# Ten operand sums of each gate and up phase on GpSimd instead of VectorE

## The chip, the cores and the metric

One Trainium2 chip, one of its cores. A core has TensorE for matmuls (PE; its weight loads are PEld), VectorE (DVE), ScalarE (ACT), GpSimd (POOL) and SyncE (SP), which issues most DMAs here. Each engine works through its own queue in order and waits on semaphores for the others. The metric is the time of one execution on the device in microseconds, lower is better, as the median of several runs.

## The reference

One layer of a hybrid decoder trunk on 1024 tokens of width 1024, all in float32:

```python
x = x + 0.5 * swiglu(rms_norm(x, ffn1_norm), ffn1_w_gate, ffn1_w_up, ffn1_w_down)
x = x + hybrid_mixer(rms_norm(x, mix_norm), w_in, ..., w_out)
x = x + 0.5 * swiglu(rms_norm(x, ffn2_norm), ffn2_w_gate, ffn2_w_up, ffn2_w_down)
return rms_norm(x, final_norm)

def swiglu(h, w_gate, w_up, w_down):
    a = jnp.einsum("bld,df->blf", h, w_gate)
    b = jnp.einsum("bld,df->blf", h, w_up)
    return jnp.einsum("blf,fd->bld", jax.nn.silu(a) * b, w_down)
```

The hidden width D_FF is 2816. The mixer (a gated delta rule of 8 heads beside a Mamba-2 scan of 16 heads) lies between the two feed-forward parts and isn't touched.

## The kernel before, in words

**Seven products.** The gate and the up matmul multiply the normalised tokens, 1024 by 1024, by weights of 1024 by 2816. The kernel cuts the tokens' matrix into four blocks (two halves of the tokens, two halves of the width) and a weight tile of 256 columns into four blocks a11, a12, a21, a22. A product of two such block matrices is made with seven block products (numbered m = 1 to 7) instead of eight; the operands of most of them are sums or differences of two blocks. The results are added up in four PSUM banks named c11, c12, c21, c22 in the code.

**High and low parts.** Each operand is split: ScalarE casts it to fp32r (the high part), VectorE subtracts the high part from it (the low part). `split2`, lines 238 to 240, does both, so one operand of 128 x 512 is a cast and a subtraction (L239, L240). A block product, `prod`, runs four steps of k with three matmuls each (L332 high by high, L333 weights' high by tokens' low, L334 weights' low by tokens' high), twelve matmuls of 512 columns.

**Names.** Token operands are `bh` and `bl`, weight operands `ah` and `al`. `wst` is a raw weight tile as loaded, `as` a weight sum, `bs` a token sum, `keepx` the two kept scaled blocks r11 and r22, `m` and `m2f` are products copied from PSUM. H[m] holds the token operand of product m, ops[m] the weight operand.

**The start of a phase.** There are two gate and up phases, one for each feed-forward part: the first starts with the kernel, the second at about 1640 us. Before the steady loop over the 22 weight tiles (11 of gate, 11 of up) a phase has a start in which all token operands are made and the first two weight tiles, one of gate and one of up, are worked on side by side:

- `b_first` (lines 261 to 269) makes the token operands 2 and 4 and keeps r11.
- `a_start` (lines 325 and 326) makes the weight operands of the first two tiles in four groups, by the table A_START: group 0 has products 2 and 4, group 1 products 3 and 6, group 2 products 5 and 7, group 3 product 1, each for both tiles. It calls `a_ops` (lines 304 to 319), where L315 is the sum of two weight blocks.
- `b_second` (lines 271 to 295) makes the token operands 3 and 6, calls `between(0)`, makes 5 (r22 alone, no sum) and 7, calls `between(1)`, and makes 1. Operands 3, 6 and 7 take one block straight from PSUM after a transpose (L279), operand 1 is the sum of the kept r11 and r22, four sums of 128 x 512 (L294).
- `between` is the function f in `start_rest` (lines 669 to 678). f(0) issues the first matmuls (`first_products`: 2, 4 and 3) and group 2 of the weights; f(1) makes group 3 and loads the next two weight tiles.
- `gate_up_all` (from line 352) goes on with products 6, 5, 7 and 1, whose bank is tagged sc, combines the banks, and enters the loop, in which `a_ops` makes the operands of the next tile by A_GROUPS.

**Buffers.** Sums and the two copies `m3` of the third product come from tag "q" of the pool, which has four buffers. The two m3 are filled early in the start and are in use until the banks are combined (lines 384 to 400). Weight operands have two buffers of four operands each, the tags whi and wlo.

**What sets the order.** The code isn't executed in the order in which it is written. A planner in the build goes through the instructions, with the written order as priority, modelled durations, and buffers given out as they come free, and writes out one queue for each engine. `tc.issue_after(ins)` puts the instructions of a block behind `ins` on its engine. In the chip each queue is then strictly in order: an instruction that waits holds everything behind it on its engine. In the second phase, for example, the planned order of TensorE has the fifth product, most of the first, and then the seventh.

Of the kernel before, what the change touches and what calls it, by code (L numbers as in the profile page):

```python
# [16 lines left out]
ALU = mybir.AluOpType  # L17
# [27 lines left out]
def kernel(  # L45
# [7 lines left out]
    V, A, G, T = nc.vector, nc.scalar, nc.gpsimd, nc.tensor  # L53
# [217 lines left out]
    def b_second(pool, x0, x1, wcol, H, r11, r22, between):  # L271

        def operand(m, k, f):
            t = pool.tile([P, 512], F32, name="bs", tag="q")
            f(t)
            return split2(b_op(H, m)[0][:, k], b_op(H, m)[1][:, k], t)

        def scaled(pt, kx, other, op):
            return lambda t: V.scalar_tensor_tensor(out=t, in0=pt, scalar=wcol[:, kx:kx + 1], in1=other,  # L279
                                                    op0=ALU.mult, op1=op)  # L280

        for k in range(4):
            A.mul(out=r22[:, k], in_=transposed(x1, k + 4), mul=wcol[:, k + 4:k + 5])
            p12 = transposed(x1, k)
            operand(3, k, scaled(p12, k, r22[:, k], ALU.subtract))
            operand(6, k, scaled(p12, k, r11[:, k], ALU.add))
        between(0)
        for k in range(4):
            split(b_op(H, 5)[0][:, k], b_op(H, 5)[1][:, k], r22[:, k])
        for k in range(4):  # L290
            operand(7, k, scaled(transposed(x0, k + 4), k + 4, r22[:, k], ALU.add))
        between(1)
        for k in range(4):
            last = operand(1, k, lambda t: V.tensor_tensor(out=t, in0=r11[:, k], in1=r22[:, k], op=ALU.add))  # L294
        return last

    A_GROUPS = ((3, 2, 1, 5), (4, 7, 6))
# [3 lines left out]
        nc.sync.dma_start(out=raw, in_=w.rearrange("(k p) c -> p k c", p=P)[:, :, p * 256:(p + 1) * 256])  # L301
        return raw

    def a_ops(pool, *prods):

        hi = wp.tile([P, 4, 4, P], F32R, name="ah", tag="whi")
        lo = wp.tile([P, 4, 4, P], F32R, name="al", tag="wlo")
        for i, (raw, m, ops) in enumerate(prods):
            a11, a12 = raw[:, 0:4, 0:P], raw[:, 4:8, 0:P]
            a21, a22 = raw[:, 0:4, P:2 * P], raw[:, 4:8, P:2 * P]  # L310
            v = {3: a11, 4: a22, 2: (a21, a22, ALU.add), 1: (a11, a22, ALU.add), 5: (a11, a12, ALU.add),
                 7: (a12, a22, ALU.subtract), 6: (a21, a11, ALU.subtract)}[m]
            if isinstance(v, tuple):
                t = pool.tile([P, 4, P], F32, name="as", tag="q")
                V.tensor_tensor(out=t, in0=v[0], in1=v[1], op=v[2])  # L315
                v = t
            last = split2(hi[:, i], lo[:, i], v)
            ops[m] = hi[:, i], lo[:, i]
        return last


    A_START = (((0, 2), (0, 4), (1, 2), (1, 4)), ((0, 3), (1, 3), (0, 6), (1, 6)),
               ((0, 5), (1, 5), (0, 7), (1, 7)), ((0, 1), (1, 1)))

    def a_start(pool, raws, ops, n):
        a_ops(pool, *((raws[j], m, ops[j]) for j, m in A_START[n]))

    def prod(H, bank, ops, m, first):
        (wh, wl), (bh, bl) = ops[m], H[m]
# [357 lines left out]
    with ExitStack() as c1:  # L687
        npool = NormPool(ffn_pools(c1))
        H = {}
        with tc.tile_pool(name="x1", bufs=1, side="right", reuse_waits="tile") as xp, \  # L690
# [5 lines left out]
            raws = [a_load(ffn1_w_gate[0], 0), a_load(ffn1_w_up[0], 0)]  # L696
            for b in range(4, NB):
                nc.sync.dma_start(out=xt[b], in_=x_v[:, b])
            ops = [{}, {}]
            x0, last = normalise_pairs(npool, xt, "h6")  # L700
            with tc.issue_after(last.ins), tc.issue_after(cols_in.ins):
                a_start(npool, raws, ops, 0)
            r11, r22 = (kp.tile([P, 4, 512], F32, name=f"keepx{i}") for i in range(2))
            with tc.issue_after(last_t.ins):
# [3 lines left out]
            last = b_second(npool, x0, x1, nrm[0], H, r11, r22,  # L708
                     start_rest(npool, H, ffn1_w_gate[0], ffn1_w_up[0], raws, ops))
# [100 lines left out]
    with tc.tile_pool(name="gtmp", bufs=1, side="right", reuse_waits="tile") as tp:  # L810
# [23 lines left out]
        for b in range(NB):  # L834
# [12 lines left out]
                        in1=bias.unsqueeze(1).to_broadcast([P, NB, NG]), op=ALU.add)  # L847
# [11 lines left out]
        for c in (15, 13, 11, 9, 7, 5, 3):  # L859
# [8 lines left out]
                               in1=alog.unsqueeze(1).to_broadcast([P, NB, NG]),  # L868
# [11 lines left out]
                        op=ALU.subtract)  # L880
# [19 lines left out]
    for un in range(4):  # L900
# [37 lines left out]
        for b0 in range(0, NB, 2):  # L938
# [6 lines left out]
            for name, lst, sc in (("xdt", xdts, bc2(dtn, b0)), ("xe", xes, bc2(dxe, b0))):  # L945
                t = s1.tile([P, 2, 256], F32, name=name, tag=name, bufs=4)
                last_x = V.tensor_tensor(out=t.rearrange("p i (h c) -> p i h c", h=4), in0=ptv, in1=sc,
                                         op=ALU.mult)
# [42 lines left out]
        for b0 in range(0, NB, 4):  # L991
# [33 lines left out]
            for b, py, *_ in pairs:  # L1025
                for j in range(2):
                    xv = xst[j][:, b * P:(b + 2) * P]
                    V.scalar_tensor_tensor(out=xv, in0=xv, scalar=dcol[:, 2 * un + j:2 * un + j + 1],
                                           in1=py[:, j * 256:(j + 1) * 256], op0=ALU.mult, op1=ALU.add)
# [71 lines left out]
    with ExitStack() as cg:  # L1101
        g1 = cg.enter_context(tc.tile_pool(name="gdn1", bufs=1, reuse_waits="tile"))
        g2 = cg.enter_context(tc.tile_pool(name="gdn2", bufs=2, reuse_waits="tile"))
        for h in range(GH):
# [31 lines left out]
            for b0 in range(0, NB, 2):  # L1136
# [14 lines left out]
                for i in range(2):  # L1151
# [4 lines left out]
                                in0=pg.rearrange("p (i c) -> p i c", i=2)[:, :, P:2 * P],  # L1156
                                in1=dt[:, b2], op=ALU.mult)
# [24 lines left out]
            for half in range(2):  # L1182
                pt = psum("mx")
                for i in range(4):
# [4 lines left out]
                                in1=rin[:, hb].unsqueeze(2).to_broadcast([P, 4, P]), op=ALU.mult)  # L1189
# [12 lines left out]
            for j in range(31):  # L1202
                r, n = j // 4 + 1, 31 - j
                t = ft[:, 0:r * n].rearrange("p (s l) -> p s l", l=n)
                V.tensor_tensor(out=t, in0=fx[:, 0:r, j:j + 1].to_broadcast([P, r, n]),
                                in1=fu[:, j:j + 1, j + 1:32].to_broadcast([P, r, n]), op=ALU.mult)
# [51 lines left out]
            for half in range(2):  # L1258
                pt = psum("sc")
                for i in range(4):  # L1260
# [4 lines left out]
                                in1=wend[:, hb, h:h + 1].to_broadcast([P, 4, P]), op=ALU.mult)  # L1265
# [3 lines left out]
            for b in range(NB):  # L1269
                bs = slice(b * P, (b + 1) * P)  # L1270
                rr = vr[:, b]
                if st is not None:
# [4 lines left out]
                                           in1=vr[:, b], op0=ALU.mult, op1=ALU.add)  # L1277
# [8 lines left out]
                if b < NB - 1:  # L1286
# [5 lines left out]
                    else:  # L1292
                        V.scalar_tensor_tensor(out=sn, in0=st, scalar=egt[:, b, h:h + 1],
                                               in1=p3[:, 0:P], op0=ALU.mult, op1=ALU.add)
# [100 lines left out]
    raws = [a_load(ffn2_w_gate[0], 0), a_load(ffn2_w_up[0], 0)]  # L1395
    ops = [{}, {}]
# [89 lines left out]
```

## Time and profile before

| | |
|---|---|
| runs | 2311.19, 2312.62, 2313.73 us; median 2312.62 |
| profiled execution | 2311.71 us |
| span of its profile | 2309.8 us, 31485 instructions |
| granted TensorE clock | 0.999 |
| PE busy | 2275.9 us, 99% |
| DVE busy | 1726.7 us, 75% |
| ACT busy | 1096.0 us, 47% |
| POOL busy | 53.6 us, 2% |
| the 220 weight sums L315 (both phases, start and loop) | 145.0 us on DVE, 684 ns each |
| the 8 token sums L294 | 692 ns each |
| GpSimd's largest work, the selections L895 | 36.5 us, 24 of them, all in the mixer |

The span runs from the first to the last instruction; the profiled execution's own time has some 1.9 us more around it. A row of a group gives line, engine, operation, output and inputs, shapes and count, then busy time in us and the mean in ns, then the idle time of the engine just before and what ended it. A row of the timeline gives start and duration in us, then engine, line, operation, and in brackets the idle time before it and its releaser; consecutive equal instructions stand in one row with their count. The matmuls are pipelined: each is shown with 0.39 us, and one starts every 0.23 us when nothing is waited for, so a busy share of TensorE near 100% can still hide holes of a few tenths. Time is lost where the distance between two starts is larger.

### The profile page before, as it was taken

How to read it: one execution, taken by the hardware profiler on the slowest of the kernel's cores; microseconds unless marked ns; L12 is line 12 of the kernel's file. 1: busy time of each engine (PE TensorE's matmuls, PEld its weight loads, DVE VectorE, ACT ScalarE, POOL GpSimd, SP SyncE). 2: the span in 40 equal slices, each digit the busy share in tenths (PEclk: the TensorE clock that was granted, in tenths of full speed). 3: DMA queues.
4: the chain of work that ended last, by engine and by line, in shares of the span. 5: the costliest groups of instructions: out<-in, count | busy, mean ns of one | idle time of the engine just before them, and what ended most of it. 6: DMA issues, size and time to landing. Idle time of an engine off the chain costs nothing.

```text
span 2309.8 us, 31485 instructions
## 1 busy us (share of the span) xinstructions
PE 2275.9 (99%) x11766; PEld 1868.7 (81%) x11766; DVE 1726.7 (75%) x3349; ACT 1096.0 (47%) x1990; POOL 53.6 (2%) x125
## 2 busy tenths in 40 slices
PE   7999999999999999999999999999999999999998
PEld 5788888888878888888888888888878888888886
DVE  7977776767765675668778888778698777766787
ACT  7433333343367785864455556422543333334344
POOL 0000000000000100000000000000000000000000
PEclk9999999999999999999999999999999999999999
DMA  3333332573652322222333222335223333329456
GB/s 111 125 114 103 105 108 98 175 279 129 220 180 78 92 92 74 72 86 74 83 101 82 73 83 61 116 98 192 91 83 116 111 102 105 109 88 349 141 156 214
DMA packets 220957, 281.33 MB, mean 122 GB/s; under 512 B 47008, under 2 KB 153564, under 8 KB 219780
## 3 DMA queue, kind: packets, MB, share of 16 engines
q1 hardware_dynamic: 220548, 279.23, 37.4%
q8 instruction: 92, 1.51, 0.3%
q14 instruction: 61, 0.50, 0.1%
q0 software_dynamic: 256, 0.10, 0.0%
HBM read 211.55 MB, written 67.73 MB: 121 GB/s over the span
## 4 chain that ended last, share of the span: by engine, by line
PE 89%; DVE 5%; ACT 2%; DMA 1%; issue 1%; SPq 0%; POOL 0%; DVEq 0%; ACTq 0%
PE ps_pj L123 11%; PE ps_pj L122 10%; PE ps_pj L121 10%; PE ps_pj L332 6%; PE ps_pj L334 6%; PE ps_pj L333 6%; PE ps_mx L332 3%; PE ps_mx L334 3%; PE ps_mx L333 3%; PE ps_pj L553 2%; PE ps_pj L554 2%; PE ps_pj L552 2%; PE ps_oo L334 2%; PE ps_oo L333 2%; PE ps_oo L332 2%; PE ps_sc L552 1%
## 5 line engine op out<-in xcount | busy, mean ns | idle before, releaser
L123 PE MATMUL ps_pj<-hhi,wlo 128*128 128x512 f32 x832 | 334.3, 402 | 0.0
L121 PE MATMUL ps_pj<-hhi,whi 128*128 128x512 f32 x832 | 332.8, 400 | 0.4 <-ACT gsb L826 0.4
L122 PE MATMUL ps_pj<-hlo,whi 128*128 128x512 f32 x832 | 332.2, 399 | 0.0
L334 PE MATMUL ps_pj<-bh,al 128*128 128x512 f32 x688 | 267.9, 389 | 0.0
L333 PE MATMUL ps_pj<-bl,ah 128*128 128x512 f32 x688 | 267.8, 389 | 0.0
L332 PE MATMUL ps_pj<-bh,ah 128*128 128x512 f32 x688 | 267.5, 390 | 0.0
L121 PEld LDWEIGHTS ps_pj<-hhi,whi 128*128 128x128 f32 x832 | 156.7, 188 | 28.8 <-ACT gsb L826 0.8
L123 PEld LDWEIGHTS ps_pj<-hhi,wlo 128*128 128x128 f32 x832 | 156.7, 188 | 28.5 <-issue 0.7
L122 PEld LDWEIGHTS ps_pj<-hlo,whi 128*128 128x128 f32 x832 | 156.7, 188 | 27.9
L239 ACT CAST ah<-wst 128x512 fp32r<-128x512 f32 x88 | 54.6, 622 | 210.8 <-PE ps_oo L333 125.3
L239 ACT CAST hid<-hraw 128x1024 fp32r<-128x1024 f32 (+1 forms) x84 | 82.3, 981 | 145.5 <-PE ps_oo L554 60.6
L333 PEld LDWEIGHTS ps_pj<-bl,ah 128*128 128x128 f32 x688 | 129.2, 188 | 26.8
L334 PEld LDWEIGHTS ps_pj<-bh,al 128*128 128x128 f32 x688 | 129.1, 188 | 26.6
L332 PEld LDWEIGHTS ps_pj<-bh,ah 128*128 128x128 f32 x688 | 128.9, 188 | 26.6
L315 DVE TENSOR_TENSOR as<-wst 128x512 f32<-128x512 f32 x220 | 145.0, 684 | 2.1 <-DMA wst<-in_ffn_w_up_dram 1.8
L240 DVE TENSOR_TENSOR al<-as,ah 128x512 fp32r<-128x512 f32 x220 | 141.0, 685 | 5.0 <-ACT ah L239 4.5
L332 PE MATMUL ps_mx<-bh,ah 128*128 128x512 f32 x352 | 138.6, 396 | 3.8 <-ACT m L341 1.4
L333 PE MATMUL ps_mx<-bl,ah 128*128 128x512 f32 x352 | 138.2, 393 | 0.4 <-DVE bl L240 0.4
L334 PE MATMUL ps_mx<-bh,al 128*128 128x512 f32 x352 | 137.7, 391 | 0.3 <-DVE al L240 0.3
L239 ACT CAST ah<-as 128x512 fp32r<-128x512 f32 x220 | 125.0, 617 | 20.8 <-DVE as L315 20.8
L240 DVE TENSOR_TENSOR hid<-hraw,hid 128x1024 fp32r<-128x1024 f32 (+1 forms) x84 | 95.0, 1131 | 32.8 <-ACT hid L239 32.5
L341 ACT COPY m<-ps_pj 128x512 f32<-128x512 f32 x88 | 51.5, 588 | 123.1 <-PE ps_pj L334 120.9
(448 smaller groups left out, 5118.9 us busy)
## 6 DMA issues: line engine op xcount, KB each, us to landing
hraw<-hid_scr SPq DMA_DIRECT2D x70, 512.0 KB, 4.4
hid_scr<-hs SPq DMA_DIRECT2D x110, 256.0 KB, 2.3
wst<-in_ffn_w_down_dram SPq DMA_DIRECT2D x50, 512.0 KB, 4.7
wst<-in_ffn_w_gate_dram SPq DMA_DIRECT2D x22, 1024.0 KB, 5.7
wst<-in_ffn_w_up_dram SPq DMA_DIRECT2D x22, 1024.0 KB, 5.4
wst<-in_w_in_dram SPq DMA_DIRECT2D x36, 512.0 KB, 5.2
hid_scr<-sg SPq DMA_DIRECT2D x44, 256.0 KB, 2.0
keep<-in_ffn_w_down_dram SPq DMA_DIRECT2D x20, 512.0 KB, 6.2
```

Source lines behind the costliest of these rows:

```text
L121: T.matmul(o, lhsT=wh, rhs=mh, start=first, stop=False)
L122: T.matmul(o, lhsT=wh, rhs=ml, start=False, stop=False)
L123: T.matmul(o, lhsT=wl, rhs=mh, start=False, stop=last)
L239: return (A.copy(out=hi, in_=src), V.tensor_tensor(out=lo, in0=src, in1=hi.bitcast(F32), op=ALU.subtract))
L240: V.tensor_tensor(out=lo, in0=src, in1=hi.bitcast(F32), op=ALU.subtract))
L315: V.tensor_tensor(out=t, in0=v[0], in1=v[1], op=v[2])
L332: T.matmul(bank, lhsT=wh[:, k], rhs=bh[:, k], start=a, stop=False, skip_group_check=True)
L333: T.matmul(bank, lhsT=wh[:, k], rhs=bl[:, k], start=False, stop=False, skip_group_check=True)
L334: T.matmul(bank, lhsT=wl[:, k], rhs=bh[:, k], start=False, stop=z, skip_group_check=True)
L341: A.copy(out=t, in_=bank)
L552: T.matmul(bank, lhsT=hh, rhs=wh, start=first and k == 0, stop=False, skip_group_check=True)
L553: T.matmul(bank, lhsT=hh, rhs=wl, start=False, stop=False, skip_group_check=True)
```

## The change

In the start of both phases, the four sums r11 + r22 of the first product's token operand are issued on GpSimd instead of VectorE, and so are the six weight sums of groups 2 and 3 of `a_start`: product 5 and product 7 for both tiles, product 1 for both tiles. That is ten sums of 128 x 512 float32 per phase, twenty in all, each with both inputs and its output in SBUF. The weight sums of groups 0 and 1 and all those of the loop stay on VectorE, as do all low parts; casts stay on ScalarE. Data, buffers and written order stay as they are.

```diff
             operand(7, k, scaled(transposed(x0, k + 4), k + 4, r22[:, k], ALU.add))
         between(1)
         for k in range(4):
-            last = operand(1, k, lambda t: V.tensor_tensor(out=t, in0=r11[:, k], in1=r22[:, k], op=ALU.add))
+            last = operand(1, k, lambda t: G.tensor_tensor(out=t, in0=r11[:, k], in1=r22[:, k], op=ALU.add))
         return last
...
-    def a_ops(pool, *prods):
+    def a_ops(pool, *prods, eng=None):
...
                 t = pool.tile([P, 4, P], F32, name="as", tag="q")
-                V.tensor_tensor(out=t, in0=v[0], in1=v[1], op=v[2])
+                (eng or V).tensor_tensor(out=t, in0=v[0], in1=v[1], op=v[2])
                 v = t
...
     def a_start(pool, raws, ops, n):
-        a_ops(pool, *((raws[j], m, ops[j]) for j, m in A_START[n]))
+        a_ops(pool, *((raws[j], m, ops[j]) for j, m in A_START[n]), eng=G if n > 1 else V)
```

## The prediction

> **What bounds the kernel now.** I read the page's busy times first, then a table of stretches around the two places where the changed instructions stand, then the instructions there in order of time.
>
> ```profile
> span 2309.8 us, 31485 instructions
> PE 2275.9 (99%) x11766; PEld 1868.7 (81%) x11766; DVE 1726.7 (75%) x3349; ACT 1096.0 (47%) x1990; POOL 53.6 (2%) x125
> ...
> 40.00:64.00 24.00, 24.00 (x121) 19.82 (x120) 23.38 (x38) 14.36 (x26) 0.00 (x0) 1.00 0.14 41
> ...
> 1676.00:1695.00 19.00, 18.50 (x90) 15.08 (x89) 18.01 (x29) 9.03 (x15) 0.00 (x0) 1.00 0.05 13
> 1695.00:1698.00 3.00, 1.57 (x6) 1.00 (x7) 2.93 (x6) 1.37 (x3) 0.00 (x0) 1.00 1.07 364
> ```
>
> The columns of the last three rows are stretch, length, then busy time of PE, PEld, DVE, ACT and POOL, the granted clock, DMA share and GB/s. TensorE bounds the kernel as a whole, so only its holes can be won. VectorE is at 75% on average, but in the stretches that hold the changed sums it is full (23.38 of 24.00, 18.01 of 19.00, 2.93 of 3.00), GpSimd is empty, and in the last one TensorE works 1.57 of 3.00 us. That is where VectorE sets TensorE's pace:
>
> ```profile
> 1694.11 0.39 PE L334 MATMUL ps_pj<-bh,al 128*128 128x512 f32 x1
> 1695.89 0.73 PE L332 MATMUL ps_sc<-bh,ah 128*128 128x512 f32 x2 [1.39 <-ACT bh L239]
> 1697.16 0.50 PE L333 MATMUL ps_sc<-bl,ah 128*128 128x512 f32 x1 [0.55 <-DVE bl L240]
> 1697.50 0.40 PE L334 MATMUL ps_sc<-bh,al 128*128 128x512 f32 x1
> ...
> 1694.49 0.69 DVE L294 TENSOR_TENSOR bs<-keepx 128x512 f32<-128x512 f32 x1
> 1695.10 0.68 DVE L240 TENSOR_TENSOR al<-as,ah 128x512 fp32r<-128x512 f32 x1
> 1695.82 0.69 DVE L294 TENSOR_TENSOR bs<-keepx 128x512 f32<-128x512 f32 x1
> 1696.42 0.68 DVE L240 TENSOR_TENSOR bl<-bs,bh 128x512 fp32r<-128x512 f32 x1
> ...
> 63.08 0.39 PE L332 MATMUL ps_oo<-bh,ah 128*128 128x512 f32 x1
> 63.31 0.39 PE L333 MATMUL ps_oo<-bl,ah 128*128 128x512 f32 x1
> 63.76 0.61 PE L332 MATMUL ps_sc<-bh,ah 128*128 128x512 f32 x2
> 64.46 0.50 PE L333 MATMUL ps_sc<-bl,ah 128*128 128x512 f32 x1
> ```
>
> A matmul that waits for nothing starts 0.23 us after the one before (63.08 to 63.31). In the second phase the first product (bank ps_sc) starts 1.55 us late, because its token sum L294 at 1694.49 and the cast behind it are late, and then waits another 0.8 us for the low part (1696.42 plus 0.68). In the first phase the same place costs 0.24 us (63.76 with two matmuls, then 64.46). So the change sits on the path in both phases, and the holes there are worth 2.4 and 0.24 us.
>
> **The change, part by part.** Per phase ten sums leave VectorE: four L315 for products 5 and 7, two L315 for product 1, four L294. Twenty in all; nothing else changes engine, no DMA moves. Each still feeds one cast on ScalarE and one subtraction L240 on VectorE. The chain of the second phase:
>
> ```profile
> 1679.31 1.89 DVE L240 TENSOR_TENSOR bl<-keepx,bh 128x512 fp32r<-128x512 f32 x3
> 1681.12 1.29 DVE L315 TENSOR_TENSOR as<-wst 128x512 f32<-128x512 f32 x2
> 1682.97 1.29 DVE L240 TENSOR_TENSOR al<-as,ah 128x512 fp32r<-128x512 f32 x2 [0.56 <-ACT ah L239]
> ...
> 1686.76 1.40 DVE L279 SCALAR_TENSOR_TENSOR bs<-ps_sc,cols,keepx 128x512 f32<-128x512 f32 x2
> ...
> 1692.44 0.69 DVE L240 TENSOR_TENSOR bl<-bs,bh 128x512 fp32r<-128x512 f32 x1
> 1693.16 0.69 DVE L315 TENSOR_TENSOR as<-wst 128x512 f32<-128x512 f32 x1
> ...
> 1674.56 0.69 ACT L283 ACTIVATE keepx<-ps_sc,cols 128x512 f32<-128x512 f32 x1
> ```
>
> A sum holds VectorE for 0.60 us: three in a row take 1.89, one alone 0.69, so the other two add 0.60 each. What a two-input sum of 128x512 costs on GpSimd this trace doesn't show. The nearest rows are its one-input selections:
>
> ```profile
> L82 POOL TENSOR_SCALAR_AFFINE_SELECT triu<-triu 128x128 f32<-128x128 f32 x1 | 0.3, 293 | 0.0
> ...
> 766.69 1.10 POOL L895 TENSOR_SCALAR_AFFINE_SELECT md<-md 128x1024 f32<-128x1024 f32 x1 [26.39 <-ACT cte L976]
> 768.59 1.23 POOL L895 TENSOR_SCALAR_AFFINE_SELECT md<-md 128x1024 f32<-128x1024 f32 x1 [0.80 <-ACT cte L976]
> ...
> 766.07 0.87 DVE L1028 SCALAR_TENSOR_TENSOR xs<-xs,dcol,ps_sc 128x256 f32<-128x256 f32 x2 [1.36 <-PE ps_sc L999]
> 766.86 2.01 DVE L977 TENSOR_TENSOR cte<-cte,ct 128x1024 f32<-128x1024 f32 x1
> 768.79 0.86 DVE L1028 SCALAR_TENSOR_TENSOR xs<-xs,dcol,ps_sc 128x256 f32<-128x256 f32 x2
> 769.91 1.21 DVE L977 TENSOR_TENSOR cte<-cte,ct 128x1024 f32<-128x1024 f32 x1
> ...
> 801.88 2.15 POOL L895 TENSOR_SCALAR_AFFINE_SELECT md<-md 128x1024 f32<-128x1024 f32 x1 [6.61 <-ACT cte L976]
> 801.84 1.23 DVE L977 TENSOR_TENSOR cte<-cte,ct 128x1024 f32<-128x1024 f32 x1 [6.82 <-ACT cte L976]
> ```
>
> 128 columns take 0.293 us and 1024 take 1.10, so a column costs 0.90 ns over a start of 0.18. Lower end: 512 columns with both inputs read at once, 0.64 us. Upper end: the two inputs read in turn, as 1024 columns, 1.10, or 1.23 as the slower row has it. I take 1.10, an estimate, since both operands have to come in. The Trainium skill, GPSIMD Engine Reference, section 3.1 (Elementwise — side-by-side cycle accounting), measures 4497 ns for a two-input add of 2048 columns; a quarter of it, 1.12 us as an estimate, would add 0.02 per sum to what follows, and no run here shows it yet.
>
> The same rows say more. L977 has both inputs in SBUF. Started 0.17 us after a selection of GpSimd it takes 2.01 us instead of 1.21: it stood still until GpSimd was done at 767.79 (0.93), and finished 1.08 later. Started 0.04 us ahead of one, it keeps its 1.23 and GpSimd takes 2.15 instead of 1.10. So the two don't overlap; who comes second waits for the whole of the first. L1028, which has one input in PSUM, takes 0.86 for two under a selection and 0.87 beside none: that kind is not held up. The Trainium skill, SBUF — State Buffer, section Who interferes with whom, states the port that the two share as an exclusive lock, against VectorE instructions with two SBUF inputs. Weighed against the trace it holds for these rows, and it speaks against this change: by it the sums come off VectorE's list but not off its time, and without it the gain would be that of the first rival below.
>
> I therefore count the sums as time in which no L240 can run, because each L240 here reads the sum (or r22) and its cast, both in SBUF. Only the four L279 of a phase have a PSUM input. **Per phase, up to the first low part of product 1** (8 of the 10 sums: four for 5 and 7, two weight sums, two L294):
>
> - longer sums: 8 x (1.10 - 0.60) = +4.0 us; ends 8 x 0.04 = +0.3 and 8 x 0.63 = +5.0.
> - L279 under GpSimd: four at about 0.70 (1.40 for two) is 2.8 us of cover at most, none if no free buffer lets a sum run then. Tag q has four buffers, and the two m3 hold one each through this stretch, so sums and L279 share two. I take half, -1.4.
> - an earlier start: on GpSimd the first sum no longer stands behind the three L240 of 1679.31, so it can start up to 1.8 us earlier (1681.12), but it shuts them out while it runs. I take half, -0.9; bounds 0 and -1.8.
> - holes of VectorE: from 1679.31 to the end of the first low part, 1697.10, are 17.8 us for 22 instructions at 0.60 and four L279 at 0.70, 16.0; 1.8 us is waiting, such as the 0.56 at 1682.97. Two engines can fill some; I take half, -0.9; bounds 0 and -1.8.
>
> That leaves +0.8 us per phase in the sum, and the slack in front of TensorE is none in either (both first low parts are waited for). **Behind it** the remaining parts of product 1 come one per sum and subtraction, 1.10 + 0.60 = 1.70 us, where they came at 1.33 (1694.49 to 1695.82) and TensorE takes six matmuls, 1.38, for each. Three more parts in the first phase: +1.0. In the second, two: +0.6, since the last part is used only behind the seventh product. Nothing is hidden here, as TensorE has no other matmul ahead in its queue.
>
> What else queues: a subtraction that waits for GpSimd holds all of VectorE behind it, and ScalarE's cast that waits for a sum holds the copies L341 that free banks. In the first phase the last low part of product 7 is ready at 60.16 and needed at 60.59, a slack of 0.43; I count nothing for it beyond the 0.8, as the delay to the first product contains it.
>
> ```profile
> 59.47 0.69 DVE L240 TENSOR_TENSOR bl<-bs,bh 128x512 fp32r<-128x512 f32 x1
> ...
> 60.59 0.39 PE L333 MATMUL ps_pj<-bl,ah 128*128 128x512 f32 x1
> ```
>
> Sum: 2 x 0.8 + 1.0 + 0.6 = +3.2 us, less than the 20 x 0.50 = 10 that the twenty sums add on the port. The profiled execution took 2311.71 us, so 2314.9; it lies 0.91 under the median of the runs, 2312.62, so 2315.8. A measurement of this kernel can tell about 0.2%, 4.6 us, from no change: under 2308.0 is faster, over 2317.2 slower.
>
> **The rivals.**
>
> *VectorE is relieved after all* (the other side). GpSimd runs the sums ahead, in its own time, where VectorE is on L279 or waiting, or its sum costs near the lower end. VectorE then has 8 x 0.60 = 4.8 us less to do before the first product, more than its lateness of 2.4 us, and both holes close: -2.6, 2310.0. For it: r11 and r22 (keepx) are complete at 1675.25 (1674.56), 19 us before the first L294, and GpSimd is empty. Against it: the two free buffers don't let sums run far ahead, and L977. It decides once a sum shuts VectorE out for less than 0.60. To be faster by over 4.6 us two more holes behind would have to close, which these sums don't set directly:
>
> ```profile
> 73.35 0.50 PE L332 MATMUL ps_mx<-bh,ah 128*128 128x512 f32 x1 [0.82 <-ACT sg L378]
> ...
> 96.11 0.50 PE L332 MATMUL ps_mx<-bh,ah 128*128 128x512 f32 x1 [0.68 <-ACT m L341]
> 97.18 0.50 PE L334 MATMUL ps_mx<-bh,al 128*128 128x512 f32 x1 [0.34 <-DVE al L240]
> ```
>
> That is 0.82 + 0.68 + 0.34 more, about 2308.2, at the edge.
>
> *The ring of two buffers makes it serial.* Sum, cast, subtraction stand one behind the other, no L279 is covered and nothing starts earlier: 2 x 4.0 + 1.6 = +9.6, 2322.2; half of the reliefs, 2319. For it: VectorE's in-order queue, and 2.15 us for a selection that lost the port once. Against it: the 1.8 us of waiting now in the stretch.
>
> *The order is worked out anew.* The build plans each queue from modelled times, and a sum on another engine shifts them. If it puts the seventh product ahead of the first in the second phase, whose token operand is ready at 1693.13 (1692.44), 12 matmuls (2.7 us) cover the hole there: about 2313. A shift elsewhere can go either way by a few us; nothing in this profile prices it.
>
> **How the numbers follow.** Forecast 52% (2315.8, its own range 2312.5 to 2319; 41 points of it within 0.2%, 11 over). Relieved 18% (12 within, 6 faster). Serial 20%, all slower. Planned anew 10% (2 faster, 7 within, 1 slower). Together faster 8%, same 60%, slower 32%. The range 2309 to 2321 reaches to the relieved case's 2310.0 and over the half-serial 2319, and leaves out the ends of both.
>
> **What would show it.** Twenty two-input sums on GpSimd of 1.1 us or, where they lost the port, up to 1.8; L240 rows near them of 1.2 to 1.8 instead of 0.69; VectorE's busy time in 1676 to 1695 not lower although ten instructions fewer; the hole before ps_sc over 1.5 us in the second phase and about 1 to 2 in the first; steps of 1.7 between the low parts. It is wrong if the L240 keep 0.69 beside GpSimd, if a sum takes under 0.7, if the hole at the first product closes, or if time moves in the stages between the two phases.

## The result, and the profile after

The changed kernel takes 2324.2 us, the median of six runs (2320.97 to 2325.3), beside 2311.29 us for the kernel before in six runs. The ratio is 1.0053, with a 95% interval from 1.004 to 1.0065. So it is slower, by 12.9 us between the medians, where the forecast added 3.2. The forecast was 2315.8 with a range up to 2321, so the time lies above the range, and even above the 2322.2 of the rival in which everything becomes serial. The profiled execution took 2323.63 us.

First the page's own lines on the kernel after:

```profile
span 2321.9 us, 31510 instructions
PE 2279.8 (98%) x11766; PEld 1871.8 (81%) x11766; DVE 1729.3 (74%) x3329; ACT 1096.9 (47%) x1990; POOL 83.3 (4%) x145
```

and one row of its table of stretches (length, then busy time of PE, PEld, DVE, ACT and POOL, the granted clock, DMA share, GB/s):

```profile
40.00:64.00 24.00, 20.28 (x91) 16.41 (x90) 19.63 (x27) 12.46 (x22) 9.91 (x6) 0.86 0.00 0
```

Twenty instructions left VectorE (3349 to 3329), and its busy time did not fall by 20 x 0.60 = 12 us; it rose from 1726.7 to 1729.3. GpSimd's rose by 29.7. A subtraction that is held up counts as busy for all the time that it takes. TensorE, which was busy in all of 40 to 64, now stands for 3.7 us there, and the granted clock is 0.86.

**Where the time went by stages.** One row of each kernel for the first and last start of the down stage's matmul L552 and of the mixer's last sum L1364, here for the kernel before:

```profile
L552 PE MATMUL ps_pj<-wd,hid x264: 387/389/479, 453.2 to 2295.7; 128*128 128x512 f32 x132
L1364 DVE TENSOR_TENSOR xt<-ps_pj,xt x24: 682/689/692, 1592.9 to 1660.8; 128x512 f32<-128x512 f32 x24
```

and for the kernel after:

```profile
L552 PE MATMUL ps_pj<-wd,hid x264: 389/389/485, 458.9 to 2307.7; 128*128 128x512 f32 x132
L1364 DVE TENSOR_TENSOR xt<-ps_pj,xt x24: 676/688/692, 1599.7 to 1667.6; 128x512 f32<-128x512 f32 x24
```

The first phase is 5.7 us later at its end (458.9 - 453.2). The mixer's end is 6.8 later; the 1.1 us between the two lie in stages that hold none of the changed sums, and from L552's first start to L1364's last the kernels of this study differ by more than that among themselves (1206.4 to 1209.6 us). From there to the last L552 another 5.2 are lost. So the loss is in the two starts, 5 to 6 us in each.

**The sums themselves**: the group of the weight sums on GpSimd, in the kernel after:

```profile
L315 POOL TENSOR_TENSOR as<-wst 128x512 f32<-128x512 f32 x12 | 19.4, 1632 | 224.5 <-DVE bl L240 221.4 <-DVE al L240 3.1
```

A sum that nothing holds up takes 1.26 to 1.29 us (the rows of both phases below), not 1.10. The weight sums have 1.63 on average: some of them take longer beside a subtraction, as in the pair of 4.67 us that GpSimd starts at 46.34 while VectorE subtracts.

**The second phase in order of time**, as the kernel after ran it: PE, then DVE, then POOL.

```profile
1705.87 0.49 PE L332 MATMUL ps_sc<-bh,ah 128*128 128x512 f32 x1 [2.30 <-ACT bh L239]
1707.67 0.50 PE L333 MATMUL ps_sc<-bl,ah 128*128 128x512 f32 x1 [1.30 <-DVE bl L240]
...
1686.10 4.07 DVE L240 TENSOR_TENSOR bl<-keepx,bh 128x512 fp32r<-128x512 f32 x3
1695.07 1.40 DVE L279 SCALAR_TENSOR_TENSOR bs<-ps_sc,cols,keepx 128x512 f32<-128x512 f32 x2
...
1705.85 6.40 DVE L240 TENSOR_TENSOR bl<-bs,bh 128x512 fp32r<-128x512 f32 x4
...
1685.82 3.20 POOL L315 TENSOR_TENSOR as<-wst 128x512 f32<-128x512 f32 x2 [168.13 <-DVE bl L240]
1700.24 3.04 POOL L315 TENSOR_TENSOR as<-wst 128x512 f32<-128x512 f32 x2 [6.47 <-DVE bl L240]
1703.91 1.26 POOL L294 TENSOR_TENSOR bs<-keepx 128x512 f32<-128x512 f32 x1 [0.63 <-DVE al L240]
1705.80 1.27 POOL L294 TENSOR_TENSOR bs<-keepx 128x512 f32<-128x512 f32 x1 [0.63 <-DVE al L240]
```

The order of the rows is as the chip ran it, with rows left out between. Three L240 in a row, 1.89 us before, take 4.07 at 1686.10, while two sums run. At the end one L294 and one L240 alternate: from 1703.91 to 1705.80 is 1.89, that is 1.26 for the sum and 0.63 in which GpSimd stands until the subtraction is done. The two engines work as if they were one. That can be added up for the stretch from 1686.10 to the end of the first low part of product 1, at about 1707.6 (TensorE starts on it at 1707.67), 21.5 us. The kernel before has 22 instructions at 0.60 there, eight of them sums; so 14 subtractions are 8.4, the four L279 at 0.70 are 2.8, and eight sums at 1.28 are 10.2: together 21.4 us, of which 0.3 lie ahead of the stretch (the first sum starts at 1685.82). All but some 0.4 us of the stretch is the work of the two engines, one after the other. What keeps them apart is not one thing: a sum holds up the subtraction beside it (4.07 for 1.89), and GpSimd waits for a subtraction to give back a buffer before the next sum (the 0.63 and the 6.47 us in brackets). No sum lies beside an L279 either: the four begin at 1695.07, and GpSimd stands idle for the 6.47 us before 1700.24.

**The first phase**, as the kernel after ran it: PE, DVE and POOL in the timeline.

```profile
56.91 1.11 PE L216 MATMUL ps_sc<-ident,xt 128*128 128x128 f32 x4 [3.72 <-DVE bs L279]
...
59.95 0.63 PE L332 MATMUL ps_pj<-bh,ah 128*128 128x512 f32 x1
60.38 0.63 PE L333 MATMUL ps_pj<-bl,ah 128*128 128x512 f32 x1
...
70.25 0.39 PE L332 MATMUL ps_sc<-bh,ah 128*128 128x512 f32 x1
72.58 0.50 PE L333 MATMUL ps_sc<-bl,ah 128*128 128x512 f32 x1 [0.58 <-DVE bl L240]
...
50.45 5.75 DVE L240 TENSOR_TENSOR al<-as,ah 128x512 fp32r<-128x512 f32 x4 [1.83 <-ACT ah L239]
56.11 1.40 DVE L279 SCALAR_TENSOR_TENSOR bs<-ps_sc,cols,keepx 128x512 f32<-128x512 f32 x2
66.91 6.44 DVE L240 TENSOR_TENSOR bl<-bs,bh 128x512 fp32r<-128x512 f32 x4
...
64.94 1.29 POOL L294 TENSOR_TENSOR bs<-keepx,keepx 128x512 f32<-128x512 f32 x1 [0.63 <-DVE al L240]
66.85 1.29 POOL L294 TENSOR_TENSOR bs<-keepx,keepx 128x512 f32<-128x512 f32 x1 [0.63 <-DVE al L240]
```

The stretch behind TensorE's wait at 56.91, with the same columns as above:

```profile
56.90:63.00 6.10, 6.09 (x19) 5.04 (x20) 4.72 (x7) 3.54 (x6) 1.69 (x1) 0.50 0.00 0
```

Here the lateness shows earlier. L279 of operand 7 stands on VectorE behind four subtractions that take 5.75 us instead of 2.4, since GpSimd's sums run between them. Transposes of operand 7 (L216) that wait for that L279 stand in TensorE's queue ahead of the rest of product 5, so TensorE waits 3.72 us. The planned order has changed here too: the transposes stand behind 6 of these matmuls on bank ps_pj, in the kernel before behind 14. After that it runs at a granted clock of 0.50: 0.43 us from matmul to matmul (59.95 to 60.38). It reaches product 1 at 70.25 instead of 63.76, and there it still waits for a low part (72.58).

### The profile page after: what moved, and what is told of

The parts are those of the page before. It is cut to its first block, busy times and chain, and to the rows that moved or that the text cites. A ratio compares the mean times of both kernels' runs of the same rounds, so it can differ in the third digit from the quotient of the medians.

```text
span 2321.9 us, 31510 instructions
## 1 busy us (share of the span) xinstructions
PE 2279.8 (98%) x11766; PEld 1871.8 (81%) x11766; DVE 1729.3 (74%) x3329; ACT 1096.9 (47%) x1990; POOL 83.3 (4%) x145
## 4 chain that ended last, share of the span: by engine, by line
PE 87%; DVE 7%; ACT 3%; DMA 2%; issue 1%; POOL 1%; SPq 0%; DVEq 0%; ACTq 0%; POOLq 0%
PE ps_pj L123 10%; PE ps_pj L121 10%; PE ps_pj L122 10%; PE ps_pj L332 6%; PE ps_pj L334 6%; PE ps_pj L333 6%; PE ps_mx L332 3%; PE ps_mx L334 3%; PE ps_mx L333 3%; PE ps_pj L553 2%; PE ps_pj L554 2%; PE ps_pj L552 2%; PE ps_oo L334 1%; PE ps_oo L333 1%; PE ps_oo L332 1%
## 5 line engine op out<-in xcount | busy, mean ns | idle before, releaser
L240 DVE TENSOR_TENSOR al<-as,ah 128x512 fp32r<-128x512 f32 x220 | 147.0, 711 | 10.6 <-ACT ah L239 9.3
L315 DVE TENSOR_TENSOR as<-wst 128x512 f32<-128x512 f32 x208 | 137.1, 682 | 2.1 <-DMA wst<-in_ffn_w_up_dram 2.1
L239 ACT CAST ah<-as 128x512 fp32r<-128x512 f32 x220 | 125.0, 618 | 26.8 <-DVE as L315 14.5
L240 DVE TENSOR_TENSOR hid<-hraw,hid 128x1024 fp32r<-128x1024 f32 (+1 forms) x84 | 94.9, 1130 | 33.1 <-ACT hid L239 32.6
L341 ACT COPY m<-ps_pj 128x512 f32<-128x512 f32 x88 | 51.5, 588 | 122.9 <-PE ps_pj L334 121.1
```

Source lines behind the costliest of these rows:

```text
L239: return (A.copy(out=hi, in_=src), V.tensor_tensor(out=lo, in0=src, in1=hi.bitcast(F32), op=ALU.subtract))
L240: V.tensor_tensor(out=lo, in0=src, in1=hi.bitcast(F32), op=ALU.subtract))
L315: (eng or V).tensor_tensor(out=t, in0=v[0], in1=v[1], op=v[2])
L341: A.copy(out=t, in_=bank)
```

## The experiments

The first theory, A, is the port: a GpSimd sum whose inputs are in SBUF and a VectorE subtraction shut each other out, so what was moved off VectorE's list stays in its time, at 1.28 us a sum instead of 0.60. The rival, B, is the ring: the buffers of tag q and the chain of sum, cast and subtraction make the work serial, and with buffers of their own the sums would run ahead and out of the way. A third, C, is TensorE's order: the transposes of operand 7 ahead of product 5, and the half clock behind that stall. The ratios below are to the kernel before on the same chip, with 95% intervals.

**The parts alone.** Three kernels each move one of the three groups of sums.

```diff
+ e1_token: only the four token sums L294 of a phase on GpSimd
+ e2_g2:    only the weight sums of products 5 and 7   (eng=G if n == 2 else V)
+ e3_g3:    only the weight sums of product 1          (eng=G if n == 3 else V)
```

> Only the four token sums of product 1 per phase are on GpSimd, all weight sums stay on VectorE. Theory A (port and queue: a GpSimd sum of 1.28 us and a VectorE subtraction with both inputs in SBUF exclude each other, and TensorE stands behind them in its planned order): the steps between the low parts of product 1 go from 1.33 to 1.9 us, no stall ahead of the transposes of operand 7, no half clock; about +1.5 us per phase, 2314 us in all (2313 to 2316). Rival B (length alone: GpSimd and VectorE overlap, and two free buffers are shared): the steps stay at 1.3 and the time at 2311. Rival C (the token sums carry most of the loss): 2320 or more.

> Only the four weight sums for products 5 and 7 per phase are on GpSimd. Theory A: this part carries most of the loss, since the transposes of operand 7 stand in TensorE's queue behind VectorE's L279, and L279 behind the subtractions that wait for GpSimd: a TensorE stall near 3.7 us in the first phase, with about 5 us at half clock behind it (2.7 us more), and near 2 us in the second, partly instead of the hole at product 1; 2318 to 2321 us. Rival B: below 2313. Rival C: 2313 to 2315.

> Only the two weight sums of product 1 per phase are on GpSimd. Theory A: +0.5 to +1.5 us per phase in front of product 1, 2312.5 to 2314. If the three parts add up, e1, e2 and e3 together give +13 us over the kernel before. Rival B: 2311.

Measured: the token sums 2316.05 us, 1.0023 (1.0014 to 1.0032); products 5 and 7 2317.41, 1.0025 (1.0016 to 1.0035); product 1's weights 2313.56, 1.0009 (1.0 to 1.0019). Above the 2311.56 of before these are 4.5, 5.9 and 2.0, together 12.3; the whole change has 12.9. None of the parts gains. The expectation held for product 1's weights alone (2312.5 to 2314); the token sums came out at the upper end of theirs (2316) and with a half clock that was not expected, products 5 and 7 below theirs (2318 to 2321). By the first L552, the ends of the first phase are 454.9, 457.5 and 453.0, that is +1.7, +4.3 and -0.2 against 453.2, together 5.8 where the whole has 5.7. That they agree so closely is in part luck, as the kernel with the memsets below, which loses nothing, has 452.0 there. From the mixer's end to the last L552 the parts lose 3.7, 1.4 and 2.4, together 7.5 where the whole has 5.2: in the second phase a part of what they lose is the same time.

Where each loses is seen in TensorE's timeline, first with the token sums alone:

```profile
64.66 0.50 PE L333 MATMUL ps_sc<-bl,ah 128*128 128x512 f32 x1 [1.34 <-DVE bl L240]
66.58 0.80 PE L333 MATMUL ps_sc<-bl,ah 128*128 128x512 f32 x1 [0.72 <-DVE bl L240]
```

The stretch behind the second of these waits, where the clock is 0.52:

```profile
67.00:70.00 3.00, 3.00 (x8) 2.29 (x8) 2.86 (x4) 1.14 (x2) 0.88 (x1) 0.52 0.04 12
```

then with products 5 and 7 alone:

```profile
56.03 1.12 PE L216 MATMUL ps_sc<-ident,xt 128*128 128x128 f32 x4 [3.71 <-DVE bs L279]
```

The token sums open the holes at product 1, and two holes of 1.34 and 0.72 are followed by half the clock (0.52 from 67 to 70). The sums of products 5 and 7 make the stall at the transposes, all of it (3.71 of 3.72). In the second phase they lose only the 1.4 us: TensorE waits 2.1 us at the transposes, and the hole at product 1 shrinks (0.60 instead of 1.39), as TensorE comes later to it.

**Is it the order on TensorE?** The whole change, with the weight sums of products 5 and 7 written behind operand 7, so that L279 no longer stands behind them.

```diff
-            a_start(pool, raws, ops, 2 + n)
             if n == 1:
+                a_start(pool, raws, ops, 2)
+                a_start(pool, raws, ops, 3)
```

> The whole change, but the weight sums for products 5 and 7 are written behind token operand 7 instead of ahead of it, so that the transposes of operand 7 and their L279 need not wait for them. Theory A: the stalls ahead of the transposes (3.72 and 2.06 us) and the half clock of the first phase go; a wait for the weights of product 5 takes some of their place: 2315 to 2320. If the loss sits in the sums' time alone, wherever they stand, the time stays near 2324.

Measured: 2323.6 us, 1.0057 (1.0042 to 1.0072), as slow as the change. TensorE's timeline:

```profile
55.12 0.80 PE L332 MATMUL ps_pj<-bh,ah 128*128 128x512 f32 x1 [2.93 <-ACT ah L239]
...
72.16 0.80 PE L333 MATMUL ps_sc<-bl,ah 128*128 128x512 f32 x1 [0.94 <-DVE bl L240]
```

The expectation of 2315 to 2320 was missed. The stall at the transposes is gone, and a wait of 2.93 us for the high part of a weight operand stands in its place; the low parts of product 1 come hardly sooner (TensorE's last wait for one ends at 72.16, beside 72.58). TensorE reaches product 1 sooner, at 67.75 instead of 70.25, and then stands three times for its low parts (0.21, 0.95 and 0.94 us). So in this order the stall of 3.72 us is no loss of its own that can be won back, and theory C falls as what sets the end of the start. The half clock follows the new waits too, so what it costs by itself is not separated. What is late is the whole list of VectorE and GpSimd.

**Is it the ring?** The whole change, with buffers of their own for eight of the ten sums of a phase (halves of token tiles that are no longer read). Two weight sums stay in the ring.

```diff
+        room[:] = [x1[i][:, 512:1024] ... for i in range(4)]
-            t = pool.tile([P, 512], F32, name="bs", tag="q")
+            t = x1[k][:, 0:512] if m == 1 else pool.tile(...)
-                t = pool.tile([P, 4, P], F32, name="as", tag="q")
+                t = room.pop(0) if eng is G and room else pool.tile(...)
```

> The whole change, but eight of the ten sums per phase get a place of their own in a dead block instead of one of the two free buffers, so that GpSimd may run ahead. Rival B (ring of two buffers): GpSimd runs its sums early, the holes close and the time goes to 2309 to 2312. Theory A (port): the sums run earlier but shut VectorE out there instead; the time stays 2316 or more.

Measured: 2323.16 us, 1.0052 (1.0037 to 1.0067). The sums do run early now, and TensorE stands elsewhere (lines are one or two further on here: L241 is the subtraction, L240 the cast, L281 the former L279, L296 the token sum, L317 the weight sum). PE, ACT and DVE:

```profile
66.58 0.50 PE L334 MATMUL ps_sc<-bh,ah 128*128 128x512 f32 x1 [2.68 <-ACT ah L240]
1691.96 0.79 PE L334 MATMUL ps_pj<-bh,ah 128*128 128x512 f32 x1 [4.84 <-ACT bh L240]
...
1689.73 0.62 ACT L240 CAST bh<-xt 128x512 fp32r<-128x512 f32 x1 [5.49 <-POOL xt L296]
...
1686.02 2.05 DVE L281 SCALAR_TENSOR_TENSOR bs<-ps_sc,cols,keepx 128x512 f32<-128x512 f32 x3
```

The time that theory B gave, 2309 to 2312, did not come: done earlier, the sums delay what VectorE makes earlier, TensorE waits at other operands, and the time is the same. But the run does not clear the ring altogether. Three L281 take 2.05 us while sums run beside them, as long as without, so the cover that the change did not get is there once sums have buffers. VectorE is almost on time again: in the first phase it comes to the first combination of the banks (L385 before, L387 here) at 68.40 us, beside 67.75 before and 73.27 with the change. What keeps the time long is elsewhere. The 2.68 us are a wait for the weights of product 1, whose two sums are those left in the ring; and in the second phase ScalarE's casts stand behind one that waits 5.49 us for a token sum. So buffers alone don't win the time back in this order; how much of the change's loss the waits for buffers make is not settled.

**The port by itself.** Two kernels that leave the change out and add work to GpSimd in the start of each phase, for which nobody waits: eight sums of r11 and r22 into dead tiles, or sixteen memsets of 128x1024 into the same tiles, which read nothing.

```diff
+        for k in range(8):      # e5_dummy
+            G.tensor_tensor(out=x1[k % 4][:, 0:512], in0=r11[:, k % 4], in1=r22[:, k % 4], op=ALU.add)
+        for k in range(16):     # e6_memset
+            G.memset(x1[k % 4], 0.0)
```

> The kernel before, with eight additional sums r11 + r22 per phase on GpSimd, written into a dead block (a used-up part of x1); nobody waits for their results and all of VectorE's work stays. Theory A (port): each additional sum holds up VectorE's subtractions, which are on the path here: subtractions of 1.2 to 1.9 us beside them, and +5 to +14 us, 2316 to 2325. Rival B (no port; the loss comes from waiting for slow sums): subtractions stay at 0.69 us and the time at 2311.

> The kernel before, with sixteen additional memsets of 128x1024 per phase on GpSimd into the same dead block: GpSimd is as busy as with the additional sums or more, but reads nothing. If it is reading that excludes VectorE: time as before, 2311. If any work of GpSimd does: subtractions held up and 2316 or more.

Measured: with the sums 2326.38 us, 1.0064 (1.0049 to 1.0079); with the memsets 2311.78, 1.0001 (0.9991 to 1.001). VectorE and GpSimd in the second phase, with the idle sums:

```profile
1688.39 5.18 DVE L240 TENSOR_TENSOR bl<-keepx,bh 128x512 fp32r<-128x512 f32 x3
...
1682.00 12.72 POOL L289 TENSOR_TENSOR xt<-keepx 128x512 f32<-128x512 f32 x8 [164.93 <-PE ps_sc L216]
```

and with the memsets:

```profile
1677.97 1.89 DVE L240 TENSOR_TENSOR bl<-bs,bh 128x512 fp32r<-128x512 f32 x3
...
1676.34 14.35 POOL L289 MEMSET xt<- 128x1024 f32 x16 [164.90 <-PE ps_sc L216]
```

Sixteen sums that no instruction waits for cost 14.5 us, 0.9 each, which is 1.4 us above the expected range of 2316 to 2325, and three subtractions take 5.18 instead of 1.89. The same engine, busy for 14.35 us with writes alone, costs nothing, and the subtractions keep their 1.89. What hurts is neither GpSimd's queue nor a wait; it is GpSimd reading SBUF while VectorE's subtractions read two operands from there. The Trainium skill, SBUF — State Buffer, section Who interferes with whom, says just this, that a VectorE instruction with two SBUF inputs contends with a GpSimd instruction that reads SBUF and not with one that only writes it. Both runs agree. The change also takes 0.60 us per sum off VectorE; by these figures the port alone would make some 20 x (0.9 - 0.6) = 6 us of its 12.9, a rough estimate, as the idle sums stand at other places and a stall of 5.0 us with half the clock behind it follows them in the second phase. The rest would then lie in what waits for the moved sums, and in the buffers.

**The forecast's hole, without the sums.** The kernel before, with product 1 put behind product 7 on TensorE, to see what the 2.4 us at product 1 in the second phase are worth.

```diff
+        with tc.issue_after(seventh.ins):
             for st in ops:
                 open_bank(H, st, "c1", 1, None, "sc")
```

> The kernel before, all sums on VectorE, with the first product put behind the seventh on TensorE by an order edge. The hole of 2.4 us at the first product of the second phase is covered by twelve to twenty-four matmuls of the seventh: 2309 if nothing else moves. If a later wait (the copies and combinations behind the first product) takes its place: 2311, as before.

Measured: 2316.73 us, 1.0022 (1.0013 to 1.0032). TensorE, and ScalarE at the end of what it waits for (L342 is the copy L341 of before):

```profile
1700.67 0.80 PE L332 MATMUL ps_pj<-bh,ah 128*128 128x512 f32 x1 [5.83 <-ACT m L342]
...
1699.52 0.62 ACT L239 CAST bh<-bs 128x512 fp32r<-128x512 f32 x1 [0.71 <-DVE bs L294]
1700.05 0.58 ACT L342 COPY m<-ps_pj 128x512 f32<-128x512 f32 x1
```

The seventh product needs the banks of the sixth, and the copy that frees them stands on ScalarE behind the casts, the last of which waits for the last token sum. Neither of the expected times, 2309 and 2311, came. The order of before is the better of the two, and the third rival's 2313 was not to be had in this way.

**Place or engine?** The kernel before, with weight sums of the steady loops on GpSimd and the starts left as they were: two per tile (products 6 and 7), then all five.

```diff
-                    made = a_ops(pool, *((raws[0], m, nxt[0]) for m in A_GROUPS[grp]))
+                    made = a_ops(pool, *(...), eng=(V, G)[grp])     # e9_loop; eng=G in e10_loop5
```

> The kernel before, with the weight sums of products 6 and 7 of the tiles inside the loop on GpSimd instead of VectorE (two per tile, 20 tiles per phase, 80 in all); the starts of both phases stay as in the kernel before. Inside the loop VectorE is busy 40.87 of 50 us in the stretch from 100 to 150 of the kernel before and TensorE has no hole. Theory port: a sum on GpSimd still costs its 1.28 us of the shared port instead of 0.60, but here the 2 x 0.68 = 1.4 us per tile of some 19 us fit in VectorE's idle time, so the time stays within 3 us of before, subtractions beside the sums are stretched to 1.2 us or more, and TensorE shows no new hole of over 0.3 us that repeats per tile. So what costs in the change is where its sums stand, not that they are on GpSimd. Rival, every sum costs its surplus wherever it stands, because the stretched subtractions are late for TensorE in the loop too: 80 x 0.68 = 54 us slower, or at a third of that 18 us. If VectorE's relief were worth anything where it has slack, the time could not be lower either, since TensorE is full there.

> The kernel before, with all the weight sums of the tiles inside the loops on GpSimd (five per tile, at most 100 per phase) instead of the two per tile of the run before; the starts stay as they were. In the stretch from 80 to 450 of the kernel before VectorE is busy 277.98 of 370 us. By the port, some 95 sums at 1.28 instead of 0.60 add 65 us to it there, 343 of 370, 93%. Theory port with slack counted over the whole loop: it still fits, the time stays within 3 us of before, though with more than twice the sums of the run before. Rival, slack counted over a tile's group: the five sums of a tile stand close together, the subtractions behind them are up to 5 x 0.68 = 3.4 us late, and where a tile has less than that to spare TensorE waits each time; at 0.5 us for each of 40 tiles +20 us. The trace would show it as repeating holes of TensorE that end with a subtraction or a cast.

Measured: two per tile 2310.67 us, 0.9992 (0.9983 to 1.0001); five per tile 2316.74, 1.0025 (1.0015 to 1.0035). GpSimd's group with two:

```profile
L315 POOL TENSOR_TENSOR as<-wst 128x512 f32<-128x512 f32 x76 | 127.8, 1702 | 851.4 <-DVE al L240 811.5 <-issue 27.3 <-PE ps_mx L334 12.5
```

VectorE in that loop:

```profile
253.97 2.98 DVE L240 TENSOR_TENSOR al<-as,ah 128x512 fp32r<-128x512 f32 x3
```

With five, the only two waits of TensorE that the view of waits shows in those loops, and the work of ScalarE at the end of the first:

```profile
99.72 0.50 PE L332 MATMUL ps_pj<-bh,ah 128*128 128x512 f32 x1 [2.81 <-ACT sg L454]
1737.61 0.50 PE L332 MATMUL ps_pj<-bh,ah 128*128 128x512 f32 x1 [2.94 <-ACT sg L454]
...
99.07 0.60 ACT L454 ACTIVATE sg<-ps_pj 128x512 f32<-128x512 f32 x1 [3.34 <-DVE m L451]
```

76 sums in the loop, nearly four times those of the change, cost nothing, though three subtractions take 2.98 there too instead of 1.89. 190 sums cost 5.6 us, about as much as the 2.81 and 2.94 of one hole in each phase, early in the loop, where TensorE waits for ScalarE's work on sg (L454), and that for VectorE (3.34 us for L451); the other tiles show none, and half the clock follows the first of them (below). With two per tile, theory A holds. With five, neither side of the expectation was met (within 3 us, or 20): slack counted over the loop holds for the loop, and the place where it runs out is its beginning alone. In these runs the price of a sum on GpSimd is paid only where VectorE sets TensorE's pace.

## Why the prediction was wrong

**The bound, and where the change sits: right.** VectorE sets the pace in both starts, and the loss lies in those two starts.

**The port: right, and shown.** The forecast counted the sums as time in which no L240 runs. The idle sums and the memsets show this by themselves, but for a small overlap (last section), and the profile after adds up by it in the second phase (all but 0.4 of 21.5 us).

**"I take 1.10": too low.** A sum takes 1.27 to 1.29 us, above the forecast's upper end of 1.23. Eight sums of a phase then add 8 x (1.28 - 0.60) = 5.4 us instead of 4.0: 1.4 of the error per phase. The rows of one-input selections did not bound a two-input sum. The estimate of 1.12 that the forecast worked out from the Trainium skill, GPSIMD Engine Reference, section 3.1, was low here by 0.16, and the measurement decides.

**The three reliefs, each taken at half: this is the step that failed most.** They were to give back 3.2 us per phase and leave +0.8 ahead of the first low part of product 1. In the second phase they gave 1.7, since that low part comes 3.7 us later in the stretch (21.5 instead of 17.8), where 5.4 were added. In the first phase they gave 0.8: the low part ends by 68.78, when the next sum starts, instead of 64.41, and the subtraction that opens the stretch starts 0.27 earlier (46.12 for 46.39), so it comes 4.6 later. One by one, in the second phase:

- "L279 under GpSimd ... I take half, -1.4": nothing. In neither phase did a sum run while one of the four L279 did; the sum at 1700.24 had to wait for a subtraction (bl L240) to give its buffer back. That cover exists is shown by the kernel with buffers of their own (2.05 us for three L281 beside sums); the buffers denied it here, which is the forecast's own bound of none.
- "an earlier start ... I take half, -0.9": 0.3. The first sum starts at 1685.82 and the subtractions at 1686.10.
- "holes of VectorE ... I take half, -0.9": 1.4, since of 1.8 us of waiting some 0.4 are left.

The forecast gave the bounds of each correctly and then chose the middle three times, as if the middles were likely for each. What it had in hand spoke against the first: it said itself that the two m3 leave two free buffers, and that none is covered if no free buffer lets a sum run then. With 1.28 a sum and the reliefs as they were, its own sum would have read +4.6 in the first phase and +3.7 in the second instead of +0.8 each.

**"1.70 us" for a step behind the first low part: 1.90.** It is the same 1.28 plus 0.63. In the second phase the last low part ends at 1712.2 (1705.85 plus 6.40); before it ended at 1700.5, and the stretch itself starts 6.8 later in the kernel after, so 4.9 us are lost. Of the first phase the last low part before was at 67.8 (66.38 plus 1.46); now it is at 73.35 (66.91 plus 6.44), 5.5 later.

```profile
66.38 1.46 DVE L240 TENSOR_TENSOR bl<-bs,bh 128x512 fp32r<-128x512 f32 x2
...
1699.08 1.46 DVE L240 TENSOR_TENSOR bl<-bs,bh 128x512 fp32r<-128x512 f32 x2
```

5.5 and 4.9 are 10.4 of the 10.9 us that the two phases lose by the stage rows (5.7 and 5.2).

**"I count nothing for it", of product 7: wrong in the trace, and of little weight in the sum.** The stall of 3.72 us and the half clock behind it were not foreseen; the forecast looked at the 0.43 us of slack of the low part, not at the transposes that stand ahead of product 5 in TensorE's queue. In the first phase TensorE alone would have been 6.5 us late at product 1 (70.25 for 63.76), while VectorE's low parts are 5.5 late: two ways to the same loss, with one cause. That moving the stall did not help is measured; how the loss of the first phase would divide if only the clock had stayed full was not tried.

**The rivals.** The serial rival, at 20%, came nearest. Its 2322.2 is 2.0 under the time, and its +9.6 is 3.3 under the 12.9, with two errors against each other: it had 1.10 for a sum, and it denied the 0.8 and 1.7 us that were relieved. Its mechanism is half of what happened: GpSimd does wait for buffers and no L279 is covered, but the idle sums, which wait for no buffer, hold up the subtractions too, and buffers of their own don't bring the time back. The relieved rival needed a sum to shut VectorE out for less than 0.60 us; it shuts it out for 1.28, and for 1.09 in the idle sums (below). Of the order worked out anew, the transposes did move ahead in the first phase; product 7 did not move ahead of product 1 in the second. The list of what would show it held for the stretched L240 and the hole of over 1.5 us at product 1 in the second phase (2.30 and then 1.30). It did not hold for VectorE's busy time from 1676 to 1695, which fell from 18.01 to 17.03 us (only over the whole kernel did it stay), for the hole of 1 to 2 us in the first (0.58), where TensorE came late itself, or for sums of 1.1 and steps of 1.7.

## What to carry to other kernels

In these runs, moving a two-input sum from VectorE to GpSimd was no relief where VectorE's own instructions also read two operands from SBUF. Count it at GpSimd's duration on a list that the two share, here 1.28 us for 0.60, ask whether a free buffer lets it run under VectorE instructions that read PSUM, and first look whether TensorE waits for that list in the stage where it stands. In a stage with slack the same move is free but wins nothing (76 sums in the loop), and at a loop's beginning it can be paid (one hole in each phase with 190 sums). When a sum of terms has several reliefs, ask for each what row shows it; a relief that only could happen is to be counted at its poor end, with the good end in the range.

## What the runs showed of the hardware that was not expected

**A sum and a subtraction overlap a little when neither waits for a buffer.** In the alternation of the kernel after, first phase, a sum starts every 1.91 us (64.94 to 66.85): its own 1.29, and 0.63 until the subtraction has given back a buffer. In the kernel with the idle sums VectorE's subtractions alternate with them without such a wait:

```profile
47.84 1.77 DVE L240 TENSOR_TENSOR bl<-keepx,bh 128x512 fp32r<-128x512 f32 x1
49.53 1.76 DVE L240 TENSOR_TENSOR bl<-bs,bh 128x512 fp32r<-128x512 f32 x1
```

One starts every 1.69 us, less than the 1.28 and 0.60 that the two take alone; with 0.60 for the subtraction, the sum costs 1.09. The forecast's 1.10 fits that by chance. The loss is exclusion, not switching; why the buffer's wait adds 0.2 us is not shown.

**Half the clock can follow waits that are short.** After the 3.72 us stall the granted clock is 0.50. But waits of 2.43 and 0.54 us, one shortly after the other, in the run with product 1's weight sums alone, brought it down as well, and the two waits of 2.81 and 2.94 us in the run with five sums per tile differ: after the first it is down, after the second it is not. The rows of the former run, from TensorE's timeline:

```profile
1695.56 0.73 PE L332 MATMUL ps_sc<-bh,ah 128*128 128x512 f32 x2 [2.43 <-ACT bh L239]
1696.84 0.50 PE L333 MATMUL ps_sc<-bl,ah 128*128 128x512 f32 x1 [0.54 <-DVE bl L240]
```

the stretch behind them:

```profile
1698.00:1701.30 3.30, 3.30 (x10) 2.61 (x9) 3.18 (x6) 1.76 (x4) 0.00 (x0) 0.51 0.67 222
```

and the two stretches behind the waits of the latter run:

```profile
99.70:103.00 3.30, 3.28 (x10) 2.65 (x11) 3.30 (x5) 1.43 (x3) 2.18 (x2) 0.67 0.97 312
1737.60:1741.00 3.40, 3.39 (x15) 2.78 (x16) 3.40 (x5) 2.00 (x4) 2.29 (x2) 1.00 0.96 291
```

The kernel before waits 1.39 and 0.55 us at the same place and keeps the full clock. Where between these the limit lies, and whether it depends on the moment of the wait, these runs don't settle. The Trainium skill, TensorE: Matmul & The Clock Gate, Part 1, gives an idle window of about 3.4 us that runs freely; the stall of 3.72 agrees with that, and the drop after 2.81 us, or after 1.34 and 0.72, is not explained by it alone.
